# Stick-breaking attention on one core: zero-padded 128-row low parts, and a causal mask by the scan and GpSimd instead of by matmuls

## The chip, the core and the metric

The kernel runs on one core of a Trainium2 chip. Five engines work side by side on it, each through its own list of instructions in program order: TensorE (PE; its weight loads are listed apart as PEld), VectorE (DVE), ScalarE (ACT), GpSimd (POOL) and SyncE (SP), which issues most DMAs. They wait for each other by semaphores. Matmuls write to PSUM, whose banks hold 128 rows of 512 float32 values. The metric is the device time of one execution in microseconds, lower is better; three runs of the kernel before were made.

## What is computed

A decoder trunk with two layers over 512 tokens and 16 learned meta tokens, model width 1024. The first layer is a state-space layer with a feed-forward part. From its output come keys and values, which the second layer's attention reads; a feed-forward part and a last norm follow. The change is in the attention alone:

```python
z = jnp.einsum('bqhd,bkhd->bhqk', qb, kb) * scale     # 16 heads of width 64
strict = s_idx < t_idx                                # only earlier keys
log_beta = jax.nn.log_sigmoid(z)
log_1m = jnp.where(strict, jax.nn.log_sigmoid(-z), 0.0)
log_remain = lax.cumsum(log_1m, axis=3, reverse=True) - log_1m
w = jnp.where(strict, jnp.exp(log_beta + log_remain), 0.0)
outs.append(jnp.einsum('bhqk,bkhd->bqhd', w, vb))
```

So a weight is sigmoid(z) of its own key times the product of sigmoid(-z) over all keys between it and the query. Everything is float32.

## The kernel before

TensorE multiplies in a reduced float32 form (F32R), so each float32 operand is split into a high part (ACT copies it) and a low part (DVE subtracts the high part). A product is then three matmuls, high by high, high by low and low by high. The weights come as tiles of 128 by 1024 (`raw`, 512 KB), are split into `wh` (ACT, L113) and `wl` (DVE, L114), and are multiplied in `mm_steps` (L135).

Tokens stand in reversed order, so that a product over later keys runs from left to right. The order of all work is written out by hand: what an engine does follows the order of the code. In the attention a grid of windows `w` of 12 steps sets it. In every step one eighth of a projection is multiplied (`all_steps`: `proj_k`, `proj_q`, `proj_v` of a pair of heads `hp`, 24 steps or two windows for a pair), and beside it stand the attention pieces of earlier heads, which `micro(w)` assigns to steps:

- `att_z(hd, i)`, i = 0, 1, 2, in steps 0, 2 and 4 of a window: the scores of 128-query blocks against their keys, packed into one PSUM bank `z` (unit 0: one block with 512 keys; unit 1: 400 and 16 keys, the 16 being meta tokens of block 0; unit 2: 272 and 144 keys). ACT takes two sigmoids, `ga` of -z and `be` of z. DVE runs the product as a scan over `ga` (L978) and multiplies `be` by it (L991).
- `att_t(hd, gi)`, one window later in steps 1, 3, 5 and 7: PE transposes `be` into PSUM (`w`, two banks), ACT and DVE split it into `wth` and `wtl`. The group gi = 1 holds the 16 meta keys, in 16 rows.
- `att_pv(hd)`, in step 11: weights times values into the bank `pv`; ACT (`ob`, L1033) and DVE (`of`, L1034) read it.

The mask is added by a matmul of the identity `idb` with a matrix `mask` of -1e30 on and above the diagonal, both in bf16 (L970), into the diagonal 128 columns of each of the four blocks of a head. K is stored with 128 rows, high part in one half and low part in the other (`khl`), and the high part of Q is stored twice (`qhh`), so that high by high and high by low are one matmul with 128 rows (L968). The low part of Q (`ql`) has 64 rows and is multiplied by the 64 rows of K's high part (L971). In `att_pv` the meta keys are two matmuls with 16 rows, for the high and the low part of the weights (L1030).

The projections use three PSUM banks `pj` in turn, K and V two each and Q one: the second bank of the next pair's K is the first bank of this pair's V, which DVE empties with L869 (`vf`). `hold` puts the first two eighths of a projection into one step.

Of the kernel before, what the change touches and what calls it, by code (L numbers as in the profile page):

```python
# [21 lines left out]
NTOK = 528  # L22
NREAL = 512
# [24 lines left out]
def trunk_kernel(ctx, tc, xu, xn, prm, octp, gvec, c_id, c_rev, c_i16, c_blk, c_mask,  # L48
                 w_glu, w_in0, w_out0, w_kv, w_q, w_o, w_in1, w_out1, out):
    nc = tc.nc  # L50
    pe, dve, act, pool, sp = nc.tensor, nc.vector, nc.scalar, nc.gpsimd, nc.sync
# [5 lines left out]
    rs_p = ctx.enter_context(tc.tile_pool(name="rs", bufs=1))  # L57
# [5 lines left out]
    ident = base.tile([128, 128], F32, tag="ident", name="ident")  # L63
# [778 lines left out]
    with ExitStack() as ax:  # L842
# [7 lines left out]
        def bank(pool_, tag):  # L850
            return pool_.tile([128, 512], F32, tag=tag, name=tag)

        mask = ac.tile([128, 128], BF16, tag="mask", name="mask")
        idb = ac.tile([128, 128], BF16, tag="idb", name="idb")
        mtmp = ac.tile([128, NTOK], F32, tag="kf", name="mtmp")
        sp.dma_start(out=mtmp[:, 0:128], in_=c_mask)
        dve.tensor_copy(mask, mtmp[:, 0:128])
        dve.tensor_copy(idb, ident)
        for j in range(1, 4):
            th, tl = (ac.tile([128, 2, NREAL], F32R, tag=f"{t}{j}", name=f"{t}{j}") for t in ("xqh", "xql"))  # L860
            xqh += [th[:, k] for k in range(2)]
# [45 lines left out]
        def proj_q(hp):  # L907
            ps = bank(pj, "pj")
            yield from hold(mm_steps([ps], xqh, xql, [(0, 0, NREAL)], split_at=1))
            qf = ac.tile([128, NTOK], F32, tag="kf", name="qf")[:, 0:NREAL]  # L910
            dve.scalar_tensor_tensor(out=qf, in0=ps, scalar=0.125, in1=rb[0][:, 0:NREAL], op0=ALU.mult, op1=ALU.mult)
            tl = qk.tile([128, NREAL], F32R, tag="ql", name="ql")
            ql[hp] = tl

            def piece(hh_):
                th = qk.tile([128, NREAL], F32R, tag=f"qh{hh_}", name=f"qh{hh_}")
                a, b = 64 * hh_, 64 - 64 * hh_
                act.activation(out=th[a:a + 64], in_=qf[a:a + 64], func=ACTF.Copy)
                act.activation(out=th[b:b + 64], in_=qf[a:a + 64], func=ACTF.Copy)
                dve.tensor_tensor(out=tl[a:a + 64], in0=qf[a:a + 64], in1=th[a:a + 64], op=ALU.subtract)  # L920
                qhh[2 * hp + hh_] = th

            for hh_ in range(2):
                later.append((now[0] + (3 + 2 * hh_ if hp else 0), lambda hh_=hh_: piece(hh_)))
            yield

        def proj_v(hp):
            ps = [bank(pj, "pj"), bank(pj, "pj")] if hp else [bank(pz, "z"), bank(pz, "z")]
            it = hold(mm_steps(ps, kvh, kvl, COLS_A, split_at=5))
            for k_ in range(KD):  # L930
                next(it, None)
                if hp == KD - 1 and 0 <= k_ - 2 < 4:
                    osplit(k_ - 2)
                if k_ < KD - 1:
                    yield
            yield from it
            vf = ac.tile([128, NTOK], F32, tag="kf" if hp else "ob", name="vf")
            scaled(vf, ps)
            def piece():
                vp0, vp1 = bank(pz, "z"), bank(pz, "z")  # L940
                for kt in range(4):
                    pe.transpose(vp0[:, 128 * kt:128 * kt + 128], vf[:, 128 * kt:128 * kt + 128], ident)
                pe.transpose(vp1[0:16, 0:128], vf[:, 512:528], ident)
                t = qk.tile([128, 5, 2, 128], F32R, tag="v", name="vhl")
                s0 = vp0.rearrange("p (k e x) -> p k e x", k=4, e=2)
                s1 = vp1[0:16, 0:128].rearrange("p (e x) -> p e x", e=2)
                act.activation(out=t[:, 0:4, :, 0:64], in_=s0, func=ACTF.Copy)
                dve.tensor_tensor(out=t[:, 0:4, :, 64:128], in0=s0, in1=t[:, 0:4, :, 0:64], op=ALU.subtract)
                act.activation(out=t[0:16, 4, :, 0:64], in_=s1, func=ACTF.Copy)
                dve.tensor_tensor(out=t[0:16, 4, :, 64:128], in0=s1, in1=t[0:16, 4, :, 0:64], op=ALU.subtract)  # L950
                vhl[hp] = t

            later.append((now[0] + 7, piece))
            yield
# [5 lines left out]

        def att_z(hd, i):
            z = bank(pz, "z")
            hp, a = hd // 2, 64 * (hd % 2)
            n = UN[i]
            for off, b, k0, nn, masked in BLOCKS[i]:
                o_ = z[:, off:off + nn]
                q0 = 128 * b
                pe.matmul(o_, lhsT=qhh[hd][:, q0:q0 + 128], rhs=khl[hd][:, k0:k0 + nn], start=True, stop=False)  # L968
                if masked:
                    pe.matmul(z[:, off:off + 128], lhsT=idb, rhs=mask, start=False, stop=False)  # L970
                pe.matmul(o_, lhsT=ql[hp][a:a + 64, q0:q0 + 128], rhs=khl[hd][a:a + 64, k0:k0 + nn], start=False, stop=True)  # L971
            be = qk.tile([128, n], F32, tag=f"be{i}", name=f"be{i}")
            ga = ac.tile([128, n], F32, tag=f"ga{i}", name=f"ga{i}")
            act.activation(out=ga, in_=z[:, 0:n], func=ACTF.Sigmoid, scale=-1.0)
            act.activation(out=be, in_=z[:, 0:n], func=ACTF.Sigmoid)

            def scan(c0, c1, init):
                dve.tensor_tensor_scan(out=ga[:, c0:c1], data0=ga[:, c0:c1], data1=ga[:, c0:c1], initial=init, op0=ALU.mult, op1=ALU.bypass)  # L978

            if i == 0:  # L980
                scan(0, n, 1.0)
                units[hd, "last"] = ga[:, 511:512]
            elif i == 1:
                scan(0, 400, 1.0)
                last = units.pop((hd, "last"))
                scan(400, 416, last)
                dve.tensor_copy(ga[:, 399:400], last)
            else:
                scan(0, 272, 1.0)
                scan(272, 416, 1.0)  # L990
            dve.tensor_tensor(out=be[:, 1:n], in0=be[:, 1:n], in1=ga[:, 0:n - 1], op=ALU.mult)  # L991
            units[hd, i] = be

        def att_t(hd, gi):
            ca, cb, cc_ = (units[hd, i] for i in range(3))
# [24 lines left out]
            dve.tensor_tensor(out=tl[0:n], in0=wp[0:n, 0:off], in1=th[0:n], op=ALU.subtract)  # L1020
            wts[hd, "t", gi] = (th, tl)

        def att_pv(hd):
            hp, hh_ = divmod(hd, 2)
            ps = bank(pp, "pv")
            seq = [(kt, i) for kt in (3, 2, 1, 0, 4) for i in range(2)]
            for j, (kt, i) in enumerate(seq):
                gi, off, n = wts[hd, kt]
                np_ = 16 if kt == 4 else 128
                pe.matmul(ps[:, 0:n], lhsT=vhl[hp][0:np_, kt, hh_, :], rhs=wts[hd, "t", gi][i][0:np_, off:off + n],  # L1030
                          start=(j == 0), stop=(j == len(seq) - 1))
# [196 lines left out]
def _pack(i):  # L1228
# [80 lines left out]
```

## Time and profile before

| | |
|---|---|
| median of three runs | 1306.22 us (1304.93 to 1306.28) |
| profiled execution, first to last instruction | 1305.2 us |
| busy in it: PE, PEld, DVE | 1241.4, 1111.8, 713.1 us |
| busy in it: ACT, POOL | 483.3, 220.4 us |
| mean granted clock of TensorE | 0.977 of 2.4 GHz |
| attention | from about 615 to 905 us |

The profile lists one execution. A line gives a start, a duration, an engine and a line of the code. Matmuls are pipelined: each is shown with its whole time through the array, so neighbours overlap, and the pace of TensorE is read from one start to the next. "Idle before" with an arrow tells how long an engine stood still before a line and what ended the wait.

### The profile page before, as it was taken

The numbers are of one execution on the slowest core, as the hardware profiler recorded it, in microseconds if no ns is written. First come the engines' busy times: TensorE is split into PE (matmuls) and PEld (weight loads), VectorE is DVE, ScalarE is ACT, GpSimd is POOL, SyncE is SP. The second block draws the span as 40 slices with busy tenths as digits, with TensorE's granted clock in tenths as the row PEclk, the third lists the DMA queues.
The fourth block names the chain that finished last, engine by engine and source line by source line (L and its number), as shares of the span: only waits on it lengthen the run. The fifth ranks groups of instructions, "written<-read, shape, count | busy, mean of one in ns | idle before, by whom it ended". The sixth has DMA issues, their size and how long they took to land.

```text
span 1305.2 us, 19835 instructions
## 1 busy us (share of the span) xinstructions
PE 1241.4 (95%) x8286; PEld 1111.8 (85%) x8286; DVE 713.1 (55%) x1029; ACT 483.3 (37%) x730; POOL 220.4 (17%) x186
## 2 busy tenths in 40 slices
PE   3679899999999999999999999999999999999996
PEld 3578899999999999999888888867788888888886
DVE  8899447633343433433887888784644444342224
ACT  5545434323232222222655555563433333321110
POOL 6444036111101110111000000002511111111110
PEclk8689999999999999999999999999999999999998
DMA  3455523232322232333211111111233223333321
GB/s 98 85 112 115 117 77 118 68 101 91 97 85 94 82 93 89 89 90 96 81 49 49 49 49 49 49 55 59 65 118 92 91 90 95 97 93 101 93 85 65
DMA packets 44774, 110.09 MB, mean 84 GB/s; under 512 B 4749, under 2 KB 17805, under 8 KB 44685
## 3 DMA queue, kind: packets, MB, share of 16 engines
q1 hardware_dynamic: 42880, 107.57, 28.9%
q8 instruction: 65, 1.06, 0.3%
q10 hardware_dynamic: 1805, 1.26, 0.3%
q14 instruction: 24, 0.20, 0.0%
HBM read 106.08 MB, written 2.74 MB: 83 GB/s over the span
## 4 chain that ended last, share of the span: by engine, by line
PE 78%; DVE 3%; ACT 1%; issue 0%; DVEq 0%; ACTq 0%
PE pgu L135 18%; PE po L135 18%; PE pu L135 10%; PE pj L135 10%; PE pg L135 10%; PE pv L1030 2%; PE pj L1071 2%; PE z L971 2%; PE w L1015 2%; PE z L968 1%; PE po L1162 1%; PE z L1071 1%; DVE xl L157 1%; DVE fo L1193 0%; DVE wl L114 0%
## 5 line engine op out<-in xcount | busy, mean ns | idle before, releaser
L114 DVE TENSOR_TENSOR wl<-raw,wh 128x1024 fp32r<-128x1024 f32 (+5 forms) x194 | 237.9, 1232 | 223.3 <-ACT wh L113 220.5
L113 ACT ACTIVATE wh<-raw 128x1024 fp32r<-128x1024 f32 (+5 forms) x194 | 189.0, 978 | 242.3 <-PE po L135 120.2
L135 PE MATMUL pgu<-xl,wh 128*128 128x512 f32 x352 | 138.7, 394 | 1.0 <-DVE xl L157 1.0
L135 PE MATMUL pgu<-xh,wh 128*128 128x512 f32 x352 | 138.4, 393 | 0.6 <-ACT xh L156 0.6
L135 PE MATMUL pgu<-xh,wl 128*128 128x512 f32 x352 | 138.5, 393 | 0.0
L135 PE MATMUL po<-hh,wh 128*128 128x264 f32 (+1 forms) x506 | 132.0, 317 | 0.0
L135 PE MATMUL po<-hh,wl 128*128 128x264 f32 (+1 forms) x506 | 131.9, 317 | 0.0
L135 PE MATMUL po<-hl,wh 128*128 128x264 f32 (+1 forms) x506 | 131.8, 317 | 0.0
L811 POOL TENSOR_TENSOR s<-s,rstd 128x528 f32<-128x528 f32 (+1 forms) x44 | 57.4, 1304 | 439.8 <-ACT s L810 439.8
L135 PE MATMUL pg<-xl,wh 128*128 128x264 f32 x536 | 109.7, 286 | 2.0 <-DVE xl L157 2.0
L135 PE MATMUL pg<-xh,wh 128*128 128x264 f32 x536 | 110.2, 287 | 1.2 <-ACT ysb L627 0.9
L135 PE MATMUL pg<-xh,wl 128*128 128x264 f32 x536 | 109.5, 286 | 0.9 <-DVE wl L114 0.9
L135 PEld LDWEIGHTS po<-hl,wh 128*128 128x128 f32 x506 | 83.3, 188 | 7.2
L135 PEld LDWEIGHTS po<-hh,wh 128*128 128x128 f32 x506 | 83.3, 188 | 7.1
L135 PEld LDWEIGHTS po<-hh,wl 128*128 128x128 f32 x506 | 83.1, 187 | 7.1
L135 PEld LDWEIGHTS pg<-xh,wh 128*128 128x128 f32 x536 | 83.5, 188 | 2.4 <-ACT ysb L627 1.6
L135 PEld LDWEIGHTS pg<-xl,wh 128*128 128x128 f32 x536 | 83.1, 188 | 2.6 <-DVE xl L157 2.6
L810 ACT ACTIVATE s<-g 128x528 f32<-128x528 f32 (+1 forms) x44 | 28.1, 638 | 154.0 <-DVE g L809 154.0
L135 PEld LDWEIGHTS pg<-xh,wl 128*128 128x128 f32 x536 | 83.3, 189 | 1.4 <-DVE wl L114 1.4
L135 PEld LDWEIGHTS pgu<-xl,wh 128*128 128x128 f32 x352 | 66.0, 188 | 17.1 <-DVE xl L157 1.7
L135 PEld LDWEIGHTS pgu<-xh,wh 128*128 128x128 f32 x352 | 66.1, 188 | 16.3 <-ACT xh L156 1.1
L135 PEld LDWEIGHTS pgu<-xh,wl 128*128 128x128 f32 x352 | 66.2, 188 | 15.0
(332 smaller groups left out, 2471.5 us busy)
## 6 DMA issues: line engine op xcount, KB each, us to landing
raw<-in_w_in SPq DMA_DIRECT2D x88, 512.0 KB, 3.7
raw<-in_w_out SPq DMA_DIRECT2D x32, 512.0 KB, 3.8
raw<-in_w_kv SPq DMA_DIRECT2D x16, 512.0 KB, 3.5
raw<-in_w_out SPq DMA_DIRECT2D x16, 384.0 KB, 3.2
m<-rd SPq DMA_DIRECT2D x8, 512.0 KB
raw<-in_w_q SPq DMA_DIRECT2D x8, 512.0 KB, 3.8
raw<-in_w_o SPq DMA_DIRECT2D x8, 512.0 KB, 3.5
op<-in_octp SPq DMA_DIRECT2D x8, 352.0 KB, 6.9
```

Source lines behind the costliest of these rows:

```text
L113: act.activation(out=wh[:, 0:nk, :], in_=r, func=ACTF.Copy)
L114: dve.tensor_tensor(out=wl[:, 0:nk, :], in0=r, in1=wh[:, 0:nk, :], op=ALU.subtract)
L135: pe.matmul(ps[pc][:, 0:n], lhsT=w[:, k, :], rhs=x[kk][:, c0:c0 + n], start=(first and k == 0 and j == 0), stop=(last and k == nk - 1 and ...
L157: dve.scalar_tensor_tensor(out=xl[k], in0=h[k][:, 0:n], scalar=g, in1=xh[k], op0=ALU.mult, op1=ALU.subtract)
L810: act.activation(out=s_, in_=g_, func=ACTF.Silu)
L811: pool.tensor_tensor(out=s_, in0=s_, in1=rstd[:, 0:n], op=ALU.mult)
L968: pe.matmul(o_, lhsT=qhh[hd][:, q0:q0 + 128], rhs=khl[hd][:, k0:k0 + nn], start=True, stop=False)
L971: pe.matmul(o_, lhsT=ql[hp][a:a + 64, q0:q0 + 128], rhs=khl[hd][a:a + 64, k0:k0 + nn], start=False, stop=True)
L1015: pe.transpose(wp[0:n, off:off + 128], src(kt, b), ident)
L1030: pe.matmul(ps[:, 0:n], lhsT=vhl[hp][0:np_, kt, hh_, :], rhs=wts[hd, "t", gi][i][0:np_, off:off + n], start=(j == 0), stop=(j == len(seq) ...
L1071: pe.matmul(ps, lhsT=w[:, k, :], rhs=x[k], start=(k == 0 and j == 0), stop=(k == KD - 1 and j == 2))
L1162: pe.matmul(ps, lhsT=w[:, k, :], rhs=x[kk][:, cs(c)], start=(i == 0 and j == 0), stop=(i == KF - 1 and j == 2))
```

## The change

The scores' low part of Q moves into tiles `qlz` of 128 rows, one per head of a pair, two sets; the other 64 rows are set to zero once, by GpSimd, so L971 (now L977) multiplies 128 rows. The meta keys' weights go into one tile `wm` of 128 rows, high part in rows 0 to 15, low part in rows 32 to 47, the rest zero; the values of the meta tokens stand twice, in the same rows of a zeroed tile `vm`. So one matmul with 128 rows takes the place of the two with 16; ACT and DVE write `vm` in two pieces each instead of one.

The matmul with the mask and its weight load go. The scan's second operation becomes a maximum, and its second input a tile `hide` with ones on the masked places of the diagonal block and zeros elsewhere; a product of sigmoids is at most 1, so masked places become exactly 1. Behind the multiplication on DVE, GpSimd multiplies the diagonal 128 columns of `be` by a tile `keep` of zeros and ones (L1001), four times for each head.

```diff
-        mask = ac.tile([128, 128], BF16, tag="mask", name="mask")
-        idb = ac.tile([128, 128], BF16, tag="idb", name="idb")
-        mtmp = ac.tile([128, NTOK], F32, tag="kf", name="mtmp")
-        sp.dma_start(out=mtmp[:, 0:128], in_=c_mask)
-        dve.tensor_copy(mask, mtmp[:, 0:128])
-        dve.tensor_copy(idb, ident)
+        keep = ac.tile([128, 128], F32, tag="keep", name="keep")
+        hide = rs_p.tile([128, NTOK], F32, tag="sq", name="hide")
+        sp.dma_start(out=keep, in_=c_mask[0])
+        pool.memset(hide[:, 128:512], 0.0)
+        sp.dma_start(out=hide[:, 0:128], in_=c_mask[1])
+        qlz = [[ac.tile([128, NREAL], F32R, tag=f"qlz{e}{j}", name="qlz") for e in range(2)] for j in range(2)]
+        vm = [ac.tile([128, 2, 128], F32R, tag=f"vm{j}", name="vm") for j in range(2)]
+        wm = ac.tile([128, 512], F32R, tag="wm", name="wm")
+        for j in range(2):
+            for e in range(2):
+                pool.memset(qlz[j][e][64 - 64 * e:128 - 64 * e].bitcast(F32), 0.0)
+            pool.memset(vm[j].bitcast(F32), 0.0)
+        pool.memset(wm.bitcast(F32), 0.0)
...
-                act.activation(out=t[0:16, 4, :, 0:64], in_=s1, func=ACTF.Copy)
-                dve.tensor_tensor(out=t[0:16, 4, :, 64:128], in0=s1, in1=t[0:16, 4, :, 0:64], op=ALU.subtract)
-                vhl[hp] = t
+                for r in (0, 32):
+                    act.activation(out=m[r:r + 16, :, 0:64], in_=s1, func=ACTF.Copy)
+                for r in (0, 32):
+                    dve.tensor_tensor(out=m[r:r + 16, :, 64:128], in0=s1, in1=m[0:16, :, 0:64], op=ALU.subtract)
+                vhl[hp] = (t, m)
...
                 pe.matmul(o_, lhsT=qhh[hd][:, q0:q0 + 128], rhs=khl[hd][:, k0:k0 + nn], start=True, stop=False)
-                if masked:
-                    pe.matmul(z[:, off:off + 128], lhsT=idb, rhs=mask, start=False, stop=False)
-                pe.matmul(o_, lhsT=ql[hp][a:a + 64, q0:q0 + 128], rhs=khl[hd][a:a + 64, k0:k0 + nn], start=False, stop=True)
+                pe.matmul(o_, lhsT=ql[hd][:, q0:q0 + 128], rhs=khl[hd][:, k0:k0 + nn], start=False, stop=True)
...
             def scan(c0, c1, init):
-                dve.tensor_tensor_scan(out=ga[:, c0:c1], data0=ga[:, c0:c1], data1=ga[:, c0:c1], initial=init, op0=ALU.mult, op1=ALU.bypass)
+                m0 = 128 if c0 == 400 else 0
+                dve.tensor_tensor_scan(out=ga[:, c0:c1], data0=ga[:, c0:c1], data1=hide[:, m0:m0 + c1 - c0], initial=init, op0=ALU.mult, op1=ALU.max)
...
             dve.tensor_tensor(out=be[:, 1:n], in0=be[:, 1:n], in1=ga[:, 0:n - 1], op=ALU.mult)
+            for off, b, k0, nn, masked in BLOCKS[i]:
+                if masked:
+                    pool.tensor_tensor(out=be[:, off:off + 128], in0=be[:, off:off + 128], in1=keep, op=ALU.mult)
...
+            if n == 16:
+                t = wm
+                act.activation(out=t[0:16], in_=wp[0:16], func=ACTF.Copy)
+                dve.tensor_tensor(out=t[32:48], in0=wp[0:16], in1=t[0:16], op=ALU.subtract)
+                wts[hd, "t", gi] = (t,)
+                return
...
-            seq = [(kt, i) for kt in (3, 2, 1, 0, 4) for i in range(2)]
+            seq = [(kt, i) for kt in (3, 2, 1, 0, 4) for i in range(1 if kt == 4 else 2)]
```

The code keeps its order, so instructions leave or join the lists but none changes places. On PE, the scores of unit 2 of one head (k and q are its keys and queries, pj the projection running beside it) stand so before:

```order
L135 MATMUL pj<-xh_2483,wl_7463 128x264 x2
L968 MATMUL z<-k_7469,qh_7600 128x272
L970 LDWEIGHTS idb
L970 MATMUL z<-mask,idb 128x128
L971 MATMUL z<-k_7469,ql 128x272
L968 MATMUL z<-k_7469,qh_7600 128x144
L970 LDWEIGHTS idb
L970 MATMUL z<-mask,idb 128x128
L971 MATMUL z<-k_7469,ql 128x144
L135 MATMUL pj<-xh_2484,wh_7462 128x264 x2
```

And in the changed kernel, at the same place:

```order
L135 MATMUL pj<-xh_2483,wl_7468 128x264 x2
L976 MATMUL z<-k_7474,qh_7601 128x272
L977 MATMUL z<-k_7474,qlz 128x272
L976 MATMUL z<-k_7474,qh_7601 128x144
L977 MATMUL z<-k_7474,qlz 128x144
L135 MATMUL pj<-xh_2484,wh_7467 128x264 x2
```

Two matmuls and their weight loads are gone, and the low parts read the padded tile. At the end of `att_pv`, still on PE, where the next pair's K projection follows, before:

```order
L1030 MATMUL pv<-wth,vhl 128x128
L1030 MATMUL pv<-wtl,vhl 128x128
L1030 MATMUL pv<-wth,vhl 128x512
L1030 MATMUL pv<-wtl,vhl 128x512
L135 MATMUL pj<-xh_2478,wh_7462 128x264
```

And in the changed kernel:

```order
L1046 MATMUL pv<-wth,vhl 128x128
L1046 MATMUL pv<-wtl,vhl 128x128
L1046 MATMUL pv<-wm,vm 128x512
L135 MATMUL pj<-xh_2478,wh_7467 128x264
```

One of the two meta-key matmuls is gone. On DVE, behind the multiplication of unit 2 in the second window of a pair, before:

```order
L991 TENSOR_TENSOR be_7573<-be_7573,ga_7574 128x415
L1020 TENSOR_TENSOR wtl<-w,wth 128x384
L920 TENSOR_TENSOR ql<-qf,qh_7600 64x512
L1020 TENSOR_TENSOR wtl<-w,wth 128x384
L114 TENSOR_TENSOR wl_7621<-raw_7387,wh_7620 128x1024
```

And in the changed kernel, with the two GpSimd multiplications of the same `be` as a sixth row, which is from GpSimd's own list:

```order
L998 TENSOR_TENSOR be_7572<-be_7572,ga_7573 128x415
L1036 TENSOR_TENSOR wtl<-w,wth 128x384
L926 TENSOR_TENSOR qlz<-qf,qh_7601 64x512
L1036 TENSOR_TENSOR wtl<-w,wth 128x384
L114 TENSOR_TENSOR wl_7622<-raw_7390,wh_7621 128x1024
L1001 TENSOR_TENSOR be_7572<-be_7572,keep 128x128 x2
```

DVE's own row order is the same; what is new is that GpSimd works beside the rows that follow the first.

## Rows read from the trace of the kernel before

**Rows 1.** Page, first part: busy time, share of the span, instructions of each engine.

```profile
PE 1241.4 (95%) x8286; PEld 1111.8 (85%) x8286; DVE 713.1 (55%) x1029; ACT 483.3 (37%) x730; POOL 220.4 (17%) x186
```

**Rows 2.** Windows view: length; busy (count) PE, PEld, DVE, ACT, POOL; clock, DMA, GB/s.

```profile
640.00:660.00 20.00, 20.00 (x123) 16.56 (x122) 18.54 (x31) 12.86 (x23) 0.00 (x0) 1.00 0.19 53
692.18:724.01 31.83, 31.83 (x203) 26.86 (x202) 25.35 (x43) 18.68 (x34) 0.00 (x0) 1.00 0.17 50
```

**Rows 3.** Timeline, PE: start, duration, line, rows*columns of weights, output, count.

```profile
701.68 0.29 PE L968 MATMUL z<-k,qh 128*128 128x272 f32 x1
...
703.23 0.29 PE L135 MATMUL pj<-xl,wh 128*128 128x264 f32 x1
...
710.20 0.28 PE L1030 MATMUL pv<-wtl,vhl 128*128 128x128 f32 x1
...
711.87 0.40 PE L968 MATMUL z<-k,qh 128*128 128x512 f32 x1
712.11 0.23 PE L970 MATMUL z<-mask,idb 128*128 128x128 bf16 x1
712.27 0.50 PE L971 MATMUL z<-k,ql 64*128 64x512 f32 x1
712.70 0.50 PE L135 MATMUL pj<-xqh,wh 128*128 128x512 f32 x1
713.03 0.39 PE L135 MATMUL pj<-xql,wh 128*128 128x512 f32 x1
```

**Rows 4.** Timeline, DVE, one pair of heads: idle time before a row in brackets.

```profile
697.28 1.23 DVE L978 TENSOR_TENSOR_SCAN ga<-ga 128x512 f32<-128x512 f32 x1 [1.65 <-ACT ga L974]
...
700.40 0.99 DVE L978 TENSOR_TENSOR_SCAN ga<-ga 128x400 f32<-128x400 f32 x1 [0.50 <-ACT ga L974]
...
705.67 0.55 DVE L1020 TENSOR_TENSOR wtl<-w,wth 128x384 fp32r<-128x384 f32 x1
...
706.74 0.27 DVE L950 TENSOR_TENSOR vhl<-z,vhl 16x128 fp32r<-16x128 f32 x1
...
711.86 0.68 DVE L1034 TENSOR_TENSOR of<-pv,ob 64x512 f32<-64x512 f32 x1 [1.11 <-ACT ob L1033]
713.43 1.23 DVE L978 TENSOR_TENSOR_SCAN ga<-ga 128x512 f32<-128x512 f32 x1 [0.89 <-ACT ga L974]
...
716.47 0.99 DVE L978 TENSOR_TENSOR_SCAN ga<-ga 128x400 f32<-128x400 f32 x1 [0.41 <-ACT ga L974]
...
719.86 1.07 DVE L978 TENSOR_TENSOR_SCAN ga<-ga 128x272 f32<-128x272 f32 x2 [0.33 <-ACT ga L974]
...
723.59 1.23 DVE L114 TENSOR_TENSOR wl<-raw,wh 128x1024 fp32r<-128x1024 f32 x1 [0.39 <-ACT wh L113]
...
725.67 0.43 DVE L869 TENSOR_TENSOR vf<-pj,rstd 128x264 f32<-128x264 f32 x1
...
729.11 1.23 DVE L978 TENSOR_TENSOR_SCAN ga<-ga 128x512 f32<-128x512 f32 x1 [1.64 <-ACT ga L974]
```

**Rows 5.** Timeline, PE: the next K projection, last row on its first bank, then second bank.

```profile
726.33 0.28 PE L135 MATMUL pj<-xh,wl 128*128 128x264 f32 x1
726.45 0.29 PE L135 MATMUL pj<-xh,wh 128*128 128x264 f32 x1
```

**Rows 6.** Timeline, DVE, in the first layer, where GpSimd works too.

```profile
211.68 4.26 DVE L114 TENSOR_TENSOR wl<-raw,wh 128x1024 fp32r<-128x1024 f32 x2 [0.24 <-ACT wh L113]
215.87 0.69 DVE L760 TENSOR_TENSOR part<-part,pg 128x528 f32<-128x528 f32 x1
```

**Rows 7.** Timeline, POOL, at the same place.

```profile
214.94 2.19 POOL L166 TENSOR_TENSOR ssq<-ssq,sq 128x528 f32<-128x528 f32 x1
```

**Rows 8.** Groups by line and shape, POOL, 20 to 40 us: count, busy us, mean ns.

```profile
L534 POOL TENSOR_TENSOR dg<-i,gv 128x128 f32<-128x128 f32 x1 | 0.4, 400 | 0.0
```

**Rows 9.** Timeline, PE, end of the attention, with the idle time before.

```profile
860.86 0.50 PE L1071 MATMUL pj<-ol,wh 128*128 128x512 f32 x1 [1.17 <-DVE ol L1066]
```

**Rows 10.** Windows view, behind that wait; the clock is the last but two.

```profile
863.00:866.00 3.00, 3.00 (x9) 2.25 (x9) 2.69 (x6) 1.52 (x4) 0.00 (x0) 0.50 0.00 0
```

More of the change, by code (lines that the diff above doesn't have):

```diff
@@ L911, in proj_q @@
             dve.scalar_tensor_tensor(out=qf, in0=ps, scalar=0.125, in1=rb[0][:, 0:NREAL], op0=ALU.mult, op1=ALU.mult)
-            tl = qk.tile([128, NREAL], F32R, tag="ql", name="ql")
-            ql[hp] = tl
             def piece(hh_):
@@ L919, in piece @@
                 act.activation(out=th[b:b + 64], in_=qf[a:a + 64], func=ACTF.Copy)
+                tl = qlz[hp % 2][hh_]
                 dve.tensor_tensor(out=tl[a:a + 64], in0=qf[a:a + 64], in1=th[a:a + 64], op=ALU.subtract)
-                qhh[2 * hp + hh_] = th
+                qhh[2 * hp + hh_], ql[2 * hp + hh_] = th, tl
             for hh_ in range(2):
@@ L943, in piece @@
                 pe.transpose(vp1[0:16, 0:128], vf[:, 512:528], ident)
-                t = qk.tile([128, 5, 2, 128], F32R, tag="v", name="vhl")
+                t = qk.tile([128, 4, 2, 128], F32R, tag="v", name="vhl")
+                m = vm[hp % 2]
                 s0 = vp0.rearrange("p (k e x) -> p k e x", k=4, e=2)
@@ L962, in att_z @@
             z = bank(pz, "z")
-            hp, a = hd // 2, 64 * (hd % 2)
             n = UN[i]
@@ L1016, in att_t @@
                     off += 128
+            if n == 16:
[4 more added lines that the diff above has]
+                return
             th = ac.tile([128, off], F32R, tag=f"wh{gi}", name="wth")
             tl = ac.tile([128, off], F32R, tag=f"wl{gi}", name="wtl")
-            act.activation(out=th[0:n], in_=wp[0:n, 0:off], func=ACTF.Copy)
-            dve.tensor_tensor(out=tl[0:n], in0=wp[0:n, 0:off], in1=th[0:n], op=ALU.subtract)
+            act.activation(out=th, in_=wp[:, 0:off], func=ACTF.Copy)
+            dve.tensor_tensor(out=tl, in0=wp[:, 0:off], in1=th, op=ALU.subtract)
             wts[hd, "t", gi] = (th, tl)
@@ L1025, in att_pv @@
             ps = bank(pp, "pv")
-            seq = [(kt, i) for kt in (3, 2, 1, 0, 4) for i in range(2)]
+            t, m = vhl[hp]
+            seq = [(kt, i) for kt in (3, 2, 1, 0, 4) for i in range(1 if kt == 4 else 2)]
             for j, (kt, i) in enumerate(seq):
                 gi, off, n = wts[hd, kt]
-                np_ = 16 if kt == 4 else 128
-                pe.matmul(ps[:, 0:n], lhsT=vhl[hp][0:np_, kt, hh_, :], rhs=wts[hd, "t", gi][i][0:np_, off:off + n],
+                pe.matmul(ps[:, 0:n], lhsT=m[:, hh_, :] if kt == 4 else t[:, kt, hh_, :], rhs=wts[hd, "t", gi][i][:, off:off + n],
                           start=(j == 0), stop=(j == len(seq) - 1))
@@ L1265, in _pack @@
     q, k = np.meshgrid(np.arange(128), np.arange(128), indexing="ij")
-    o["c_mask"] = np.where(k <= q, f(-1e30), f(0)).astype(f)
+    o["c_mask"] = c(np.stack([k > q, k <= q])).astype(f)
     def pw(w, order=None):
```

## Prediction

> **What bounds the kernel now.** I read the page's first part, then the attention by windows, then the timelines of PE and DVE over one pair of heads. The page says TensorE: PE is busy for 95% of the span, DVE for 55% [rows 1]. That is an average over stages, and the change is worth what it is worth in its own stage. In the attention a pair of heads takes 31.83 us, and PE is busy for all of it [rows 2]. But DVE is busy for 25.35 of the 31.83 there, and for 18.54 of the first 20 us [rows 2]. So PE sets the pace now, and DVE is next, with 6.48 us a pair to spare. Whatever PE saves beyond that cannot show. ACT has 13 us to spare, GpSimd does nothing at all.
>
> **What PE saves.** Prices are differences of start times in [rows 3]. The mask matmul takes 712.11 to 712.27, 0.16. The matmul with 64 rows takes 712.27 to 712.70, 0.43, where 512 columns with 128 rows take 0.24 (711.87 to 712.11): 0.19 more. The matmul behind it takes 0.33, 0.10 more than that. So a change of shape on the way in and out costs about 0.29 in all, and is gone when every matmul has 128 rows. Unit 0 takes 711.87 to 713.03, 1.16, and would take three steps of 0.23, 0.69: 0.47 saved. Unit 1, with one mask, one such pair of shape changes, and a 16-column piece: 0.16 + 0.29 + 0.10 = 0.55. Unit 2 takes 701.68 to 703.23, 1.55, and has 2 x (272 + 144) columns and the one projection step of x2; at the pace of 128-row matmuls about 0.71: 0.84 saved. `att_pv`'s last piece takes 710.20 to 711.87, 1.67: one 128-column and four 512-column steps' time, 0.11 + 4 x 0.23 = 1.03, would be left: 0.64. Together 2.5 a head, 5.0 a pair, 40 us for 16 heads. If PE alone mattered the time would be 1306 - 40 = 1266.
>
> The first of these prices stands on one rule as well. The Trainium skill, TensorEngine Tiling (Array Packing), Key Properties, says that a change of the tiling mode drains TensorE; by that rule the padded tiles save the drains, and the 0.19 and 0.10 of [rows 3] agree. The same page's Overview holds that a contraction of 64 rows or fewer underuses the array and gains from tiles; that speaks against padding, but only where two tiles run side by side, and no run here shows that.
>
> **What DVE then allows.** The timeline of DVE over a pair [rows 4] shows where its 6.48 us stand. Waits of 0.50, 0.41, 0.33 and 0.89 us are for `ga`, 1.11 for `ob`, 0.39 for `wh`; together 3.63. All of these come from work that PE does earlier once it is 5 us a pair faster, so I let them close. About 1.2 us are steps of 0.03 to 0.13 between dependent DVE instructions, which stay. The last wait, 1.64 us before the scan at 729.11, is a loop that DVE itself closes: `vf`'s first half ends at 725.67 + 0.43 = 726.10 and empties the bank into which the next K's second half goes; PE starts there at 726.45 [rows 5], then does unit 0's scores, ACT takes `ga`, and DVE's scan starts: 3.01 us after `vf`. Of this go the 0.35 that PE comes late (I take 0.30), the mask's 0.16, and 0.11 by which a 128-row matmul is shorter than the 64-row one (0.39 against 0.50 [rows 3]): 0.57. DVE gets 0.19 more for the second piece of `vm` (the 0.27 row in [rows 4], which starts 0.19 before the row behind it).
>
> **What GpSimd's multiplications cost.** None stands in the attention before. The nearest row is one over 128x128 in the first layer, 0.40 us [rows 8]; eight a pair are 3.2 us of an engine that is idle, and the transposes that read `be` come a window later, so their own time is hidden with 12 steps of cover. What may be lost is DVE's time beside them. In the first layer two `wl` subtractions, each with two inputs in SBUF, took 4.26 us [rows 6], where one alone takes 1.23 [rows 4]: 0.90 more each, beside GpSimd's 2.19 us of work at 214.94 [rows 7]. The next DVE row there, with one operand in PSUM, took 0.69 beside the same GpSimd work [rows 6], its ordinary time. So the price depends on what DVE does just behind the multiplication of `be`. Below: nothing. Above: the whole 0.40 for each of eight, 3.2 a pair. By the order, units 0 and 1 are followed by a `wtl` or `qf`, which read PSUM; unit 2, with two multiplications of 0.80 together, by a `wtl` of 0.55 [rows 4] and then, in one window of two, by the `qlz` subtraction with two SBUF inputs. So once a pair some 0.25 to 0.40 remain to collide; I take 0.35, nearer to nothing than to 3.2.
>
> The Trainium skill, SBUF — State Buffer, Who interferes with whom, says that a DVE instruction with two SBUF inputs contends with a GpSimd instruction that reads SBUF, that the lock is held for a whole instruction, and that DVE with one SBUF input does not contend. [rows 6] agree. By that rule alone the order decides, and the sum stays as above.
>
> **The rest at nothing.** GpSimd's memsets are about 3,500 columns of a row; at the price of the 0.40 for 128 columns [rows 8], an upper bound, 11 us once, in a stretch where GpSimd has nothing else to do, while the weights of the first pair are still being multiplied. A scan that takes a maximum reads a second tile where the old one was given `ga` twice. No row shows such a scan; the old form already names two inputs, so I price it at nothing, and the other bound is that it runs at half its pace, another 1.23 + 0.99 + 1.07 = 3.3 us a head [rows 4], which would make the kernel slower (counted with E). ACT's second piece of `vm`, about DVE's 0.27, lies in ACT's 13 us of slack. `hide` comes by a DMA that waits for GpSimd's last use of its tile, and `raw` loads stand behind it on SP's queue; those are issued well ahead of their splits, and without that cover it would cost a few us once.
>
> **The sum.** A pair saves 3.63 + 0.57 - 0.19 - 0.35 = 3.66, so 31.83 becomes 28.2, and PE stands still for some 1.3 us a pair at the second bank of K. Five whole pairs: 18.3. The pair before the tail has no projection of a next K to wait for: 0.50 + 1.11 + 0.89 - 0.19 = 2.3. The first 20 us, where DVE is at 93% [rows 2]: 0.7. The casts of the mask on DVE ahead of it: 0.2. The tail's `ol` waits, where PE already stands 1.17 us for DVE [rows 9]: nothing. Scores of the last head (0.47 + 0.55 + 0.84) and the `att_pv` next to it (0.64), on a path of PE for the most part: 2.0 of the 2.5. The last three `att_pv`: 3 x 0.6 = 1.8. Sum 25.3. The profiled execution's span is 1305.2, the median 1306.22, so 1.0 lies around the span and stays: 1306.2 - 25.3 = **1281 us**.
>
> **The rivals.** Within 0.2% (2.6 us) is what a measurement of this kernel can't tell from no change.
>
> *A, DVE and the loop over K's second bank take over after 3 to 4 us a pair*, as summed: 1274 to 1286. Chance 0.52.
>
> *B, PE stays the bound.* The loop's 1.64 shrinks too, and 13 to 16 of the 16 heads save their 2.5: 33 to 40 us, 1266 to 1273. Against it: 25.35 + 0.19 of DVE's work and 1.2 us of steps stand against a PE pair of 26.85. Chance 0.17.
>
> *C, half the gain goes.* Either every multiplication on GpSimd holds DVE up by its own 0.40, 3.2 a pair in place of 0.35, so about 6 x 2.85 = 17 of the 25 are lost; or 64-row matmuls cost what they do for another reason, and only the 64 masks of 0.16 go, 10 us; or PE's new stalls bring the clock down. The half clock (0.50 granted, 1.2 GHz) stands in this stage only behind PE's wait of 1.17 us for `ol` [rows 9, 10]; stalls of 1.3 us at K's second bank are as long, and a stretch of 3 us at half clock does 1.5 us' work. In six pairs that is 9 us. 1287 to 1303. Chance 0.21.
>
> *D, no change to be told* because the change frees PE where it must wait for DVE at once: 0.05. Against it: 3.63 us of DVE's waits that PE ends.
>
> *E, slower.* Each multiplication holds DVE like the two in [rows 6], 0.90: eight a pair are 7.2, against the 3.66 + 0.35 saved, so +3.2 a pair, six pairs +19, 1325. It decides from 4.0 / 8 = 0.50 us a multiplication. For it: DVE's next row would have to be one with two SBUF inputs, at nearly every place; by the order it is so at one or two of eight. Chance 0.05.
>
> **How the numbers follow.** The likeliest is A, 1281. Its own bounds are 1274 to 1286. The range reaches into B (to 1268) and C (to 1293): outside stand 0.07 of B, 0.03 to 0.08 of C's upper part, D and E with 0.10; about 0.2. Faster by over 0.2%: A, B, C, 0.90; within: 0.05; slower: 0.05.
>
> **What would show it.** Right: no 64-row or 16-row matmul among the scores; unit 0 at about 0.7 us from start to start; a pair at about 28 us with DVE busy for over 25 of it and no wait for `ob`; PE idle before the second bank of K, released by `vf`; GpSimd rows of 0.4 beside PSUM rows of normal length. Wrong: a pair at 27 with PE never idle (B); `wtl`, `qlz` or `wl` rows lengthened by 0.4 or more behind `be` (C, E); granted clock under 1.00 within the pairs (C); a scan row longer than 1.23 for 512 columns.

## The result, and the profile after

The changed kernel takes 1288.16 us (median of four runs, 1287.10 to 1290.03), the kernel before 1305.97 beside it: a ratio of 0.9865, 95% interval 0.9851 to 0.9879. That is 17.8 us faster, where 25.3 were forecast; it lies in the stated range of 1268 to 1293, but above rival A's own bounds of 1274 to 1286. The profiled execution took 1287.1 us with a span of 1285.3, 19.9 less than the one before.

The attention by stages shows where they went. This is the windows view of the changed kernel, cut at the starts of scans over 512 columns: start of the kernel; first head; five pairs of heads; the pair before the tail; the next two scans; the rest. Columns as in [rows 2].

```profile
0.00:640.15 640.15, 591.56 (x4975) 580.54 (x4976) 345.97 (x487) 226.37 (x340) 154.29 (x144) 0.96 0.35 94
640.15:667.02 26.87, 22.92 (x144) 20.50 (x143) 22.23 (x35) 15.21 (x27) 6.40 (x8) 0.94 0.20 59
667.02:809.03 142.01, 135.82 (x957) 126.20 (x956) 128.49 (x215) 94.25 (x171) 28.34 (x40) 1.00 0.19 57
809.03:839.63 30.60, 29.43 (x199) 26.44 (x197) 29.28 (x48) 24.30 (x45) 4.07 (x8) 1.00 0.18 52
839.63:851.85 12.22, 8.67 (x37) 6.32 (x37) 11.15 (x21) 5.29 (x12) 2.11 (x4) 0.86 0.21 60
851.85:1285.30 433.45, 419.07 (x1904) 341.10 (x1902) 179.97 (x231) 119.04 (x148) 72.18 (x54) 0.99 0.29 87
```

And the same stages of the kernel before, the first left out:

```profile
639.99:665.41 25.42, 25.42 (x156) 20.99 (x155) 21.73 (x35) 15.16 (x27) 0.00 (x0) 1.00 0.22 63
665.41:824.66 159.25, 159.25 (x1008) 134.39 (x1006) 126.97 (x210) 93.41 (x166) 0.00 (x0) 1.00 0.16 50
824.66:857.60 32.94, 32.94 (x202) 27.07 (x200) 28.77 (x47) 22.76 (x41) 0.00 (x0) 1.00 0.17 49
857.60:870.16 12.56, 11.39 (x48) 7.92 (x48) 10.58 (x20) 6.65 (x15) 0.00 (x0) 0.86 0.24 67
870.16:1305.20 435.04, 422.68 (x1910) 342.62 (x1909) 179.45 (x231) 119.14 (x148) 69.53 (x50) 0.99 0.28 87
```

From the lengths, after against before: five pairs 17.24 us shorter (18.3 forecast), the pair before the tail 2.34 (2.3), the next scans 0.34 (0), the rest 1.59 (3.8). The stage of the first head got 1.45 longer, where 0.7 less was forecast, and the start 0.16 longer. In the pairs TensorE, busy throughout before, now stands still for 6.2 of 142 us; its clock is 1.00 there.

One pair in the windows view, which answers to the second of [rows 2]:

```profile
695.45:723.84 28.39, 27.13 (x193) 25.21 (x192) 25.70 (x43) 18.84 (x35) 5.67 (x8) 1.00 0.19 56
```

TensorE's work fell from 31.83 to 27.13, DVE's rose from 25.35 to 25.70, and the pair takes 28.39: more than either. What sets it stands in two timelines of the changed kernel. PE at unit 0 and at the second bank of K, which answer to [rows 3, 5]:

```profile
707.82 0.40 PE L976 MATMUL z<-k,qh 128*128 128x512 f32 x1
708.06 0.39 PE L977 MATMUL z<-k,qlz 128*128 128x512 f32 x1
708.29 0.39 PE L135 MATMUL pj<-xqh,wh 128*128 128x512 f32 x1
708.52 0.40 PE L135 MATMUL pj<-xql,wh 128*128 128x512 f32 x1
...
721.34 0.39 PE L135 MATMUL pj<-xh,wh 128*128 128x264 f32 x1 [1.26 <-DVE vf L876]
721.57 0.29 PE L135 MATMUL pj<-xl,wh 128*128 128x264 f32 x1
```

DVE, end of one pair and start of the next (to hold against [rows 4]):

```profile
680.50 0.68 DVE L1050 TENSOR_TENSOR of<-pv,ob 64x512 f32<-64x512 f32 x1
681.22 1.22 DVE L985 TENSOR_TENSOR_SCAN ga<-ga,hide 128x512 f32<-128x512 f32 x1
...
689.12 0.70 DVE L926 TENSOR_TENSOR qlz<-qf,qh 64x512 fp32r<-64x512 f32 x1
689.75 0.54 DVE L1036 TENSOR_TENSOR wtl<-w,wth 128x384 fp32r<-128x384 f32 x1
690.22 1.21 DVE L114 TENSOR_TENSOR wl<-raw,wh 128x1024 fp32r<-128x1024 f32 x1
691.45 0.84 DVE L926 TENSOR_TENSOR qlz<-qf,qh 64x512 fp32r<-64x512 f32 x1
692.43 0.43 DVE L876 TENSOR_TENSOR vf<-pj,rstd 128x264 f32<-128x264 f32 x1
...
720.85 0.43 DVE L876 TENSOR_TENSOR vf<-pj,rstd 128x264 f32<-128x264 f32 x1
...
723.84 1.22 DVE L985 TENSOR_TENSOR_SCAN ga<-ga,hide 128x512 f32<-128x512 f32 x1 [1.63 <-ACT ga L980]
```

The reader sees unit 0 at 708.52 - 707.82 = 0.70 us (0.69 forecast); `of` and the scan behind it with no wait, where 1.11 and 0.89 stood; and one wait left on DVE, 1.63 before the pair's first scan. PE waits 1.26 us for `vf`. From `vf`'s end (721.28) to the scan 2.56 us pass, 2.44 forecast. The scan over two tiles takes what the old one took.

The first head is the surprise. GpSimd and DVE there in the changed kernel, and the waits of PE in 640 to 668 us (in all, times, longest):

```profile
649.77 2.30 POOL L1001 TENSOR_TENSOR be<-be,keep 128x128 f32<-128x128 f32 x2 [3.87 <-DVE be L998]
```

```profile
649.10 0.59 DVE L998 TENSOR_TENSOR be<-be,ga 128x415 f32<-128x415 f32 x1
649.73 0.70 DVE L907 TENSOR_TENSOR k<-kf,k 64x528 fp32r<-64x528 f32 x1
650.46 1.37 DVE L985 TENSOR_TENSOR_SCAN ga<-ga,hide 128x512 f32<-128x512 f32 x1
651.93 0.69 DVE L998 TENSOR_TENSOR be<-be,ga 128x511 f32<-128x511 f32 x1
653.27 0.69 DVE L1036 TENSOR_TENSOR wtl<-w,wth 128x512 fp32r<-128x512 f32 x1 [0.65 <-ACT wth L1035]
655.43 0.99 DVE L985 TENSOR_TENSOR_SCAN ga<-ga,hide 128x400 f32<-128x400 f32 x1 [1.46 <-ACT ga L980]
```

```profile
PE w L1025 <- POOL be L1001: 2.1, 1, 2.1
PE w L1025 <- DVE be L998: 1.8, 1, 1.8
```

Two multiplications, 0.46 each elsewhere, take 2.30: `k` and the scan, with two inputs in SBUF, stand right behind `be` on DVE. The transposes of this head come four steps after its unit 2 (step 9 of one window, step 1 of the next), where later heads have nine. So PE waits for GpSimd, the granted clock is 0.57 on average from 652 to 656 us, mostly its lower level of 1.2 GHz (0.91 over 640 to 660), and DVE then waits for PE.

### The profile page after: what moved, and what is told of

Same layout as the page of the kernel before. It is cut to its first block, busy times and chain, and to the rows that moved or that the text cites. A ratio compares the mean times of both kernels' runs of the same rounds, so it can differ in the third digit from the quotient of the medians.

```text
span 1285.3 us, 19786 instructions
## 1 busy us (share of the span) xinstructions
PE 1207.5 (94%) x8206; PEld 1101.1 (86%) x8206; DVE 717.1 (56%) x1035; ACT 484.5 (38%) x738; POOL 267.4 (21%) x258
## 3 DMA queue, kind: packets, MB, share of 16 engines
q10 hardware_dynamic: 1805, 1.26, 0.3%
## 4 chain that ended last, share of the span: by engine, by line
PE 66%; DVE 13%; issue 1%; ACT 1%; POOL 0%; DVEq 0%; ACTq 0%
PE pgu L135 19%; PE po L135 18%; PE pu L135 10%; PE pg L135 10%; DVE ga L985 3%; PE pj L135 3%; DVE wl L114 2%; PE pj L1087 2%; DVE wtl L1036 1%; DVE be L998 1%; PE po L1178 1%; DVE qlz L926 1%; PE z L1087 1%; DVE xl L157 1%; DVE k L907 1%
## 5 line engine op out<-in xcount | busy, mean ns | idle before, releaser
L1001 POOL TENSOR_TENSOR be<-be,keep 128x128 f32<-128x128 f32 x64 | 43.6, 691 | 192.1 <-DVE be L998 187.6
```

The lines of the kernel that those rows point to most:

```text
L1001: pool.tensor_tensor(out=be[:, off:off + 128], in0=be[:, off:off + 128], in1=keep, op=ALU.mult)
```

## The experiments

Each ratio is to the kernel before, with its 95% interval. A pair's time is the distance between two first scans in the profile.

**Padding alone**, the mask by matmuls as before (the lines are changes to the changed kernel):

```diff
+                if masked:
+                    pe.matmul(z[:, off:off + 128], lhsT=idb, rhs=mask, start=False, stop=False)
...
-                dve.tensor_tensor_scan(out=ga[:, c0:c1], data0=ga[:, c0:c1], data1=hide[:, m0:m0 + c1 - c0], initial=init, op0=ALU.mult, op1=ALU.max)
+                dve.tensor_tensor_scan(out=ga[:, c0:c1], data0=ga[:, c0:c1], data1=ga[:, c0:c1], initial=init, op0=ALU.mult, op1=ALU.bypass)
...
-                    pool.tensor_tensor(out=be[:, off:off + 128], in0=be[:, off:off + 128], in1=keep, op=ALU.mult)
```

> Padded tiles as in the changed kernel, mask by matmul as before. Theory (in the changed kernel DVE, and its loop from vf over K's second bank to the first scan, sets a pair's 28.4 us, so the masks' matmuls are worth next to nothing on top of the padding): TensorE alone would need 31.83 - 2 x (2.5 - 0.64) = 28.1 us a pair, the loop gets 0.16 back and loses the collision with GpSimd, so a pair takes 28.3 to 28.6; the two waits of TensorE at 650 us of the changed kernel, one of them for GpSimd, shrink; 1284 to 1288 us. Rival (the two halves of the change add up): the masks carry a quarter of the gain, a pair takes 29.3 us, 1292 to 1294 us.

Measured: 1284.34 us, ratio 0.9823 (0.9807 to 0.9840), a pair 28.38. The intervals of this and of the whole change don't overlap: half of the change is faster than all of it. At the first head the second and third scan over 512 columns stand 14.13 us apart (650.78 to 664.91), where the changed kernel has 16.56 (650.46 to 667.02). Its windows row for a pair, and its PE at unit 0:

```profile
693.24:721.62 28.38, 27.97 (x201) 25.43 (x200) 25.57 (x43) 18.90 (x35) 0.00 (x0) 1.00 0.18 56
```

```profile
705.89 0.40 PE L977 MATMUL z<-k,qh 128*128 128x512 f32 x1
706.13 0.23 PE L979 MATMUL z<-mask,idb 128*128 128x128 bf16 x1
706.17 0.48 PE L980 MATMUL z<-k,qlz 128*128 128x512 f32 x1
706.49 0.39 PE L135 MATMUL pj<-xqh,wh 128*128 128x512 f32 x1
```

TensorE has 0.84 us more to do than in the changed kernel, and the pair is as long: the bound is elsewhere. And the mask's matmul takes 0.04 from start to start, where 0.16 stood in [rows 3]; the matmul behind it takes 0.32 in place of 0.23.

**The mask alone**, with the 64-row and 16-row matmuls of before (changes to the kernel before):

```diff
-                if masked:
-                    pe.matmul(z[:, off:off + 128], lhsT=idb, rhs=mask, start=False, stop=False)
...
+                dve.tensor_tensor_scan(out=ga[:, c0:c1], data0=ga[:, c0:c1], data1=hide[:, m0:m0 + c1 - c0], initial=init, op0=ALU.mult, op1=ALU.max)
...
+                    pool.tensor_tensor(out=be[:, off:off + 128], in0=be[:, off:off + 128], in1=keep, op=ALU.mult)
```

> Mask by the scan and GpSimd as in the changed kernel, low parts of Q and meta weights in 64 and 16 rows as before. Theory: TensorE stays the bound and saves four masks of 0.16 us a head, 1.28 a pair, so a pair takes 30.5 to 30.6 us, with GpSimd's work hidden; at the first head 1 to 2 us are lost where the transposes wait for GpSimd; 1296 to 1299 us. Rival (GpSimd's multiplications hold up DVE by 0.4 each): 3.2 us a pair eat DVE's spare time of 3.6, a pair takes 31.5 or more, 1304 us or more.

Measured: 1307.38 us, ratio 1.0003 (0.9994 to 1.0013), a pair 31.31. The theory's 1296 to 1299 fell. The rival's time is nearer, by another way than it says: TensorE is busy for all of the 31.31, so DVE holds nothing up. PE at unit 0 of this kernel shows why:

```profile
715.43 0.40 PE L967 MATMUL z<-k,qh 128*128 128x512 f32 x1
715.76 0.49 PE L968 MATMUL z<-k,ql 64*128 64x512 f32 x1
716.18 0.50 PE L135 MATMUL pj<-xqh,wh 128*128 128x512 f32 x1
```

The first matmul now takes 0.33 where it took 0.24: the step from 128 to 64 rows costs about 0.1 in the matmul ahead of it too, and the mask's 0.16 held this 0.1. Taking the mask away saves 0.07, not 0.16; eight a pair are 0.56, and 31.83 - 31.31 = 0.52 was measured. The first head pays it back. This kernel's PE and GpSimd there:

```profile
651.74 0.47 PE L1016 MATMUL w<-ident,be 128*128 128x128 f32 x1 [2.05 <-POOL be L992]
```

```profile
649.38 2.30 POOL L992 TENSOR_TENSOR be<-be,keep 128x128 f32<-128x128 f32 x2 [3.87 <-DVE be L989]
```

From the scan at 650.07 to that at 669.66 us passed 19.59 us, at a mean granted clock of 0.83, against 15.18 before (650.23 to 665.41).

**Without GpSimd's multiplications** (the weights of masked places stay in the output):

```diff
-                    pool.tensor_tensor(out=be[:, off:off + 128], in0=be[:, off:off + 128], in1=keep, op=ALU.mult)
```

> The changed kernel without GpSimd's multiplications by keep (the weights of masked places are not set to zero). Theory: in a pair they cost only what one qlz row is longer by, 0.15 us, so a pair takes 28.2 to 28.3; at the first head the wait for GpSimd at 650 us and the half clock behind it go, 2 us; 1284 to 1286 us. Rival (GpSimd holds DVE up by 0.4 at each): a pair takes 27.0 or less and 1276 us or less.

Measured: 1284.13 us, ratio 0.9825 (0.9811 to 0.9840), a pair 28.21; the scans at the first head stand 14.01 us apart (649.68 to 663.69) in place of 16.56. As the theory had it: GpSimd costs 0.18 a pair and 2.5 us at the first head.

**Each multiplication twice:**

```diff
-            for off, b, k0, nn, masked in BLOCKS[i]:
+            for off, b, k0, nn, masked in BLOCKS[i] * 2:
```

> The changed kernel with each multiplication by keep done twice (the weights are the same). Theory: GpSimd's work hides but where DVE's rows with two SBUF inputs meet it, so a pair goes from 28.4 to 28.5 to 29.0 us, and the wait at the first head grows by 1 to 3 us; 1290 to 1294 us. Rival (each multiplication holds DVE up by 0.4): a pair takes 31 to 32 us, 1305 us or more.

Measured in a single run, so without an interval: 1294.86 us, a pair 28.95, the first head's scans 18.69 apart. Eight more multiplications cost 0.56 a pair, 0.07 each.

**The late `qlz`**: the piece of a pair's second head goes behind `vf` and `of`. For that `vf` gets a buffer of its own, and `qlz` one set in place of two:

```diff
-            vf = ac.tile([128, NTOK], F32, tag="kf" if hp else "ob", name="vf")
+            vf = ac.tile([128, NTOK], F32, tag="vf" if hp else "ob", name="vf")
...
-                later.append((now[0] + (3 + 2 * hh_ if hp else 0), lambda hh_=hh_: piece(hh_)))
+                later.append((now[0] + (3 + 6 * hh_ if hp else 0), lambda hh_=hh_: piece(hh_)))
```

> The changed kernel with vf in a buffer of its own, and the qlz piece of a pair's second head (one DVE subtraction, two copies on ACT) four steps later, behind vf and of. Theory: vf stands 0.85 to 1.0 us earlier in DVE's list, its loop over K's second bank shortens by as much, and DVE's wait of 1.63 before the first scan takes up the subtraction: a pair takes 27.4 to 27.6 us, 1282 to 1284 us. Rival (TensorE, ACT or DVE's whole work binds, and the wait only moves): a pair stays within 0.2 of 28.4, 1287 to 1289 us.

Measured: 1280.87 us, ratio 0.9804 (0.9789 to 0.9818), a pair 27.30, a little less than the theory's in both. The last rows of a pair on DVE:

```profile
719.67 0.42 DVE L876 TENSOR_TENSOR vf<-pj,rstd 128x264 f32<-128x264 f32 x1
720.01 0.41 DVE L877 TENSOR_TENSOR vf<-pj,rstd 128x264 f32<-128x264 f32 x1
720.35 0.67 DVE L1050 TENSOR_TENSOR of<-pv,ob 64x512 f32<-64x512 f32 x1
721.05 0.69 DVE L926 TENSOR_TENSOR qlz<-qf,qh 64x512 fp32r<-64x512 f32 x1
722.64 1.23 DVE L985 TENSOR_TENSOR_SCAN ga<-ga,hide 128x512 f32<-128x512 f32 x1 [0.89 <-ACT ga L980]
```

`qlz` fills the idle time, the wait shrinks from 1.63 to 0.89, and TensorE, with 27.12 of 27.30 us, sets the pace again. This is the loop by which the prediction worked, shown by shortening it.

**The first head's scores earlier:**

```diff
-                put(z, (0, 2, 4) if z else (3, 6, 9), (), None)
+                put(z, (0, 2, 4) if z else (2, 4, 6), (), None)
```

> The changed kernel with the scores of the first head at steps 2, 4 and 6 of their window in place of 3, 6 and 9. Theory (the first head's last be is multiplied only four steps ahead of the transposes, and GpSimd waits there for DVE's two-input rows, so TensorE waits 1.85 and 2.05 us and falls to half clock): with more steps between, both waits and the half clock at 652 us go, from the scan at 650 to that at 667 us passes 14.1 us in place of 16.6; 1285 to 1286.5 us. Rival (DVE, busy for 93% there, is the bound and the waits only move): 16 us or more, 1287 to 1289 us.

Measured: 1286.49 us, ratio 0.9836 (0.9820 to 0.9853); the scans stand 14.19 apart, no half clock is left there, and GpSimd is gone from PE's waits. The stretch answers to the theory; the interval of the whole time just overlaps with the changed kernel's.

**Both edits together**, and **both with padding alone** (the mask by matmuls):

> Both edits that helped or should help: the second head's qlz behind vf and of, and the first head's scores at steps 2, 4 and 6. Theory: they act at different places and add up, pair 27.3 us, 1278 to 1279 us. Rival (the stall at the first head doesn't depend on the steps): 1281 us as with the late qlz alone.

> As the run before, but with the mask by matmuls and without GpSimd's multiplications. Theory: with the loop over vf shortened, TensorE's own need decides, 27.97 us a pair with the masks against 27.13 without, so the masks' matmuls, worth nothing in the changed kernel's pairs, now cost 0.7 to 0.9 a pair: 28.0 to 28.2 us a pair, 1281.5 to 1284 us. Rival (DVE's 25.6 us and its steps are the bound): a pair as in the run before, 27.3 us, and 1279 us or less.

Measured: 1280.13 us, ratio 0.9785 (0.9770 to 0.9800), a pair 27.28; and 1280.32 us, ratio 0.9788 (0.9773 to 0.9802), a pair 27.80. The two windows rows, with GpSimd's mask and with the matmuls:

```profile
691.74:719.02 27.28, 27.12 (x193) 25.20 (x192) 25.45 (x44) 18.82 (x35) 5.67 (x8) 1.00 0.20 61
```

```profile
691.86:719.66 27.80, 27.80 (x201) 25.38 (x200) 25.60 (x43) 18.91 (x35) 0.00 (x0) 1.00 0.19 57
```

Both are faster than the changed kernel, and not to be told from each other. The first came out 1 us above its theory, the second 1 us below. By the whole time the first is not to be told from the late `qlz` alone either; the first head's scans, 13.09 us apart (651.37 to 664.46) where the late `qlz` alone has 16.12 (651.95 to 668.07), show that its rival is wrong. In the second a pair lies between theory and rival: TensorE is busy for all of it, but needs 27.80, not 27.97, and the masks' matmuls cost 0.5 a pair. The profiles, 1278.5 and 1279.8 us long, show why little of that is seen in the whole time: in five pairs the second is 2.66 us longer, but up to them it is 0.43 shorter and behind them 0.93, which leaves 1.3. The medians are 0.2 apart; the second's profiled run was the slowest of its four.

**Each half of the padding alone**, added to the kernel before: the meta keys' tile, or `qlz` (one set), in each case with its part of the change's diff and nothing else.

> The kernel before with the meta keys' weights in one zero-padded tile, and nothing else of the change. From the steps in the run with padding alone, the end of the weights-by-values product takes 0.39 us in place of 0.87, and 0.1 may go behind it: 0.5 to 0.6 a head, so a pair, still bound by TensorE, takes 30.6 to 30.9 us; 1296 to 1299 us. By the prediction's 0.64 a head: 30.55 and 1296. Rival (the 16-row matmuls are hidden or cost little): 31.5 us or more.

> The kernel before with the low part of Q in zero-padded tiles (one set, two tiles), and nothing else of the change; the mask stays a matmul. Theory (a matmul with 64 rows makes its neighbours dear on both sides, the mask's matmul among them, which takes 0.04 us between matmuls of 128 rows and 0.16 beside one of 64): 1.3 to 1.45 us a head, a pair takes 28.9 to 29.3 us, 1285 to 1289 us, and TensorE hardly waits. Rival (the prediction's sharing out: the mask's 0.16 is its own, and padding the scores saves 2.5 - 0.64 - 0.64 = 1.2 a head): a pair takes 29.4 us or more.

Measured: 1303.39 us, ratio 0.9971 (0.9955 to 0.9986), a pair 31.08; and 1286.33 us, ratio 0.9849 (0.9821 to 0.9878), a pair 28.88 with TensorE busy for all of it. The meta tile gives less than expected, 0.75 a pair in place of 1.0 to 1.2. Its timeline shows where the rest went: the end of `att_pv` and the matmuls behind it got shorter by 0.57 a head, as expected, but at K's second bank, where PE now comes 0.06 us after `vf`, 0.36 a pair is lost (0.38 from the first bank's last row to it in place of 0.12, and 0.23 for its own first row in place of 0.13). So the loop over `vf` holds here already. The tile of Q's low part gives 2.95 a pair, as the theory had it; with it alone the kernel is as fast as with the whole change (two runs, and the intervals overlap).

## Why the prediction came out as it did

**The number.** 1288.16 lies in the range, but outside the bounds of rival A, which was called the likeliest, and inside those of C (1287 to 1303). In the pairs the mechanism is A's all the same. Of C's three causes two did not come: GpSimd does not hold DVE up by 0.40 a multiplication, and the 64-row matmuls save what padding was to save. The third, a fall of the clock behind new stalls, came at the first head and not at K's second bank, where PE waits 1.26 us and the clock stays at 1.00. That the range held the time is owed to its reach into C: the larger misses (first head, tail, five pairs) all lie on one side.

**What bounds.** Right. PE paced the pairs before; after, a pair takes 28.39, with a wait for `vf` at the second bank of K, and the late `qlz` showed that the loop decides: 1.1 us shorter by moving one DVE row (and two copies on ACT).

**What PE saves.** The sum was near (4.70 a pair, 5.0 forecast), its sharing out wrong, so the nearness is in part luck. The step "The mask matmul takes 712.11 to 712.27, 0.16" put on the mask what belongs to the 64 rows beside it: taken away alone it gives 0.07, and between matmuls of 128 rows, where it takes 0.04 and the matmul behind it 0.09 more, the masks cost 0.84 a pair, 0.1 each. So padding is 3.9 to 4.2 of the 4.7, and the masks are 0.5 to 0.8, where 1.3 was forecast. The Trainium skill's rule that a change of tiling mode drains TensorE (TensorEngine Tiling (Array Packing), Key Properties) agrees with all three spacings, 0.04, 0.16 and 0.33 for 0.24; read with it, the 0.16 of a 128-column matmul ahead of a 64-row one might have looked too dear to be its own.

**What DVE allows.** Right but for sizes. The 3.63 us of waits closed. The loop gave 0.45 in place of 0.57 (3.01 to 2.56): behind its wait PE's first row on K's second bank takes 0.23 (721.34 to 721.57), where it took 0.13 before (726.45 to 726.58). The second `vm` piece took 0.38, not 0.19, read as in [rows 4] from one start to the next (0.57 for two pieces, 0.19 for one):

```profile
704.48 0.56 DVE L959 TENSOR_TENSOR vm<-z,vm 16x128 fp32r<-16x128 f32 x2
705.05 0.43 DVE L876 TENSOR_TENSOR kf<-pj,rstd 128x264 f32<-128x264 f32 x1
```

The collision with GpSimd took 0.18 (28.39 against 28.21 without it), not 0.35. With these sizes a pair would save 3.52; it saved 3.44 (the 0.08 between are in the steps between DVE's rows), and 3.66 were forecast. Misses on both sides cancel in that.

**What GpSimd costs.** In the pairs less than forecast, because mostly GpSimd waits for DVE and not DVE for GpSimd: once a pair its two multiplications of unit 2 take 2.93 us beside `qlz` and `wl`, 0.89 in the other window, and of DVE's rows only the second `qlz` is clearly longer, 0.84 for 0.69. The prediction knew only DVE's price for meeting GpSimd, from [rows 6], and asked what is behind `be` on DVE; it did not ask who waits for GpSimd. (It also put that price down to the one GpSimd row of [rows 7], which starts at 214.94, a microsecond before the two `wl` end; the trace has two more, from 211.53 and 212.94, beside them. None of the sum's terms hangs on it.) The step that failed is "the transposes that read `be` come a window later, so their own time is hidden with 12 steps of cover": it is nine steps in most heads and four for the first, DVE's next rows there have two SBUF inputs, and it cost 2.5 us with the half clock behind it. With the 0.7 that was to be saved there, the stage of the first head accounts for 2.2 of the 5.4 us by which the profile's 19.9 fall short of 25.3.

**The tail.** The second step that failed is "on a path of PE for the most part": of 3.8 us there, 1.93 came, 1.59 in the last stage and 0.34 in the one before, where the last head's unit 0 stands. PE's waits at the end of the attention, in the changed kernel:

```profile
842.90 0.53 PE L1087 MATMUL pj<-ol,wh 128*128 128x512 f32 x1 [2.93 <-DVE ol L1082]
...
860.41 0.55 PE L1025 MATMUL w<-ident,be 128*128 128x128 f32 x3 [1.64 <-DVE wtl L1036]
868.72 0.55 PE L1025 MATMUL w<-ident,be 128*128 128x128 f32 x3 [0.89 <-DVE wtl L1036]
```

The first stood at 1.17 in [rows 9]; as the prediction said of these waits, what PE saves ahead of it brings nothing. The last two stood at 0.30 and 0.36 before, so 1.87 us of what PE saves in the last heads went into waiting for DVE to empty the transposes' banks, which is all that is missing from the 3.8. That is read from the trace; no run was made on it, so as a cause it is argued and not shown.

**The rest.** Pairs short by 1.1 us in five, and the start by 0.36, make up the sum; what the start lost was not followed up. Of the other 2.1 us between the profile's 19.9 and the medians' 17.8, half is the spread of the four runs: the profiled one, 1287.10, was the fastest, 1.06 below the median. The other half lies in the prediction's step "1.0 lies around the span and stays": in every later run that has both figures, 29 of them of the kernel before, 1.7 to 2.1 us lie around the span. The profiled execution of the kernel before, whose time is not on record, so took about 1307.0 (an estimate from its span of 1305.2 and 1.8), 1.0 above the median of 1305.97; the prediction had given it 1306.2.

## What to carry to other kernels

Read what a matmul costs from its neighbours too: a matmul with 64 or 16 rows among matmuls of 128 made the ones ahead of it and behind it dearer by about 0.1 us each, and padding with zero rows took 3.9 us a pair off TensorE's 31.8, while taking away the matmul that seemed to cost 0.16 gave 0.07. When an engine gives up work, find the loop through another engine that holds it next, and move that engine's rows off it: one DVE row moved was worth 1.1 us a pair, while the whole second half of the change, the mask, was worth nothing there beside the padding (28.39 against 28.38) until that row was moved (27.28 against 27.80). Work handed to an idle engine must be asked for its tightest reader, which stood here at the start of the pipeline, not in its steady part.

## What the hardware showed that was not expected

GpSimd can be kept out for longer than one instruction of DVE. Its two multiplications of unit 2, as its timeline shows them in the two windows of a pair:

```profile
688.82 2.93 POOL L1001 TENSOR_TENSOR be<-be,keep 128x128 f32<-128x128 f32 x2 [2.59 <-DVE be L998]
...
703.58 0.89 POOL L1001 TENSOR_TENSOR be<-be,keep 128x128 f32<-128x128 f32 x2 [3.12 <-DVE be L998]
```

The Trainium skill, SBUF — State Buffer, Who interferes with whom, has a DVE row with at most one SBUF input free of contention, and the lock held for an instruction at a time; by that the second multiplication, which by its timeline starts at 689.24 and is 0.46 long elsewhere, could have had its turn while DVE worked on the `wtl` at 689.75, which has one input in PSUM. But it takes 2.51 and ends at 688.82 + 2.93 = 691.75, only when `qlz` (689.12), that `wtl` and `wl` (690.22 to 691.43), back to back on DVE, are done. The rows agree in that the multiplication, which started after `qlz`, was the one that waited, and DVE lost little; that it did not end within the 0.4 us between two DVE rows with two SBUF inputs differs, and the cause is open.
